# A hybrid backbone step on one core: the first layer's adaLN vectors 2 to 4 on VectorE, the mLSTM gate in another part of Y, another order of the first loads and another last LayerNorm

## The chip, the cores and the metric

The kernel runs on one core of a Trainium2 chip. The core has TensorE (PE; its weight loads are listed apart as PEld), VectorE (DVE), ScalarE (ACT), GpSimd (POOL) and SyncE (SP); each runs its own list of instructions in order and waits on semaphores where data come from another engine or from a transfer. In this kernel SP issues nearly all DMAs, in one order. The metric is the device time of one execution in microseconds.

## The reference, cut to what matters

Two layers (D = 1024) on 640 tokens: 128 prompt tokens and 512 sample tokens, in five tiles of 128 (tile 0 is the prompt). Everything is float32. Shortened from the reference, for one layer:

```
s1, b1, g1, s2, b2, g2 = adaLN(silu(cond))      # 6 vectors of 1024, for 2 conditions
                                                # (prompt, samples): cond @ ada_w + ada_b
h  = x * (1 + scale1) + shift1
aq, ak, av, bq, bk, bv, cq, ck, cv, co, cg = split(h @ w_in)
A  = diff_attention(aq, ak, av)                 # 4 heads, two maps; cached keys and values
B  = neighbourhood / dense attention(bq, bk, bv)  # 4 heads; cached keys and values
C  = head_rms(mLSTM(cq, ck, cv, cg)) * sigmoid(co)  # both directions, 4 heads
x  = layer_norm(ALPHA * x + gate1 * ([A B C] @ w_out))
h  = x * (1 + scale2) + shift2
x  = layer_norm(ALPHA * x + gate2 * (relu(h @ w1)**2 @ w2))
```

The six adaLN vectors of a layer are numbered 0 to 5 here. Vectors 0 and 1 are needed before the first projection of the layer, 2 (the gate of the attention residual) before its out projection, 3 and 4 before the MLP, 5 at the end of the MLP.

## The kernel before, in words

**Products.** A float32 product is made of three matmuls on a high and a low part of each operand (`mul3`, lines 98, 99, 100). Weights come from HBM as chunks of 1 MB into one of two buffers `raw`; ScalarE copies the high part of a quarter (L172) and VectorE subtracts it to get the low part (L117), into one of two or three `wt` slots. The cached keys of group A go the same way (`cak` by DMA, `AK` by L1066 and L117).

**Order.** `layer` writes a plan: a list of `Unit`s, each with a function that emits instructions, a cost in TensorE cycles, and the weight chunks it needs. `weave` merges lists of units in proportion to their costs; `run` walks through the plan and puts chunk loads and splits between the units, in the order in which the plan needs the chunks (`try_dma`, L210). A list scheduler of the language then sets the final order of each engine from the program and its own estimates. So moving one unit moves neighbours on all engines.

**Stages of a layer.** adaLN, the projection of group C, then `c_attn` (mLSTM) woven with `b_proj` (projection of group B), then `a_proj` (projection of group A) woven with `b_attn`, then group A's attention, the out projection, LayerNorm, the MLP in eight chunks of 512 hidden columns, LayerNorm. `Y` is a tile of 128 x 5 x 1024 that is used by all of them in turn: in `c_proj` the mLSTM gate sigmoid(co) is kept in columns 0 to 255 (`sink_o`, `sigm`), `combine` multiplies head outputs `hs` with it into columns 768 to 1023, and `b_attn` loads its own values (from the scratch tensor `s_bv`, L942) and the cached ones (`cbv`, L943) into columns 0 to 511.

**adaLN before.** In layer 0 vectors 0 and 1 are made first of all, by TensorE (`ada_units`: per chunk 16 matmuls of line 380 with `condS` as the moving operand, a copy to `adpart`, 4 picks of line 389, then line 392 on VectorE). Their eight chunks have buffers of their own (`ada`, five of them); `first_units` loads them, the tokens `x`, and the first two `w_in` chunks in four quarters, and multiplies quarter by quarter. Vectors 2 to 4 of layer 0 are twelve more such units, woven into `a_proj` and `b_attn` and the heads behind them. Vector 5 and all of layer 1's are made by VectorE (`ada_dve`, L426: four ops per chunk, each 128 x 1024 by a broadcast row `condB`, summed along the row) between the units of layer 0's MLP.

**The other places.** `rpow` (L127, L128) is a two-step power on GpSimd. `bm` are the six bias tiles of the neighbourhood scores, made on GpSimd (L952) and added on VectorE (L976). `s_aq` is a scratch tensor for the rotated queries of group A (L1090 to L1092 make them, L1116 stores them). In the last layer the final LayerNorm of a token tile is lines 1494 and 1495 (residual), 1366 and 1367 (statistics), `rpow`, 1499 and 1500.

Of the kernel before, what the change touches and what calls it, by code (L numbers as in the profile page):

```python
# [6 lines left out]
F32 = mybir.dt.float32  # L7
F32R = mybir.dt.float32r
AF = mybir.ActivationFunctionType
ALU = mybir.AluOpType  # L10
# [32 lines left out]
PACK = (("abT", (DEPTH, 48)), ("lnT", (DEPTH, 4, KT)), ("ident", (P,)), ("sel2", (2,)),  # L43
        ("cosT", (4, 64)), ("sinT", (4, 64)), ("nmask", (3, 32)), ("gA", (DEPTH,)), ("gC", (DEPTH, 2)))

# [23 lines left out]
class Step:  # L69
# [61 lines left out]
    def w_src(self, k):  # L131
# [4 lines left out]
        if kind == "adt":  # L136
            return d["adaT"][j + (4 if l else -20)]
# [150 lines left out]
    def setup(self):  # L288
# [14 lines left out]
        nc.sync.dma_start(self.condS, d["cond"])  # L303
        pack = self.pack = c.tile([P, d["pack"].shape[1]], F32, name="pack")
# [10 lines left out]
        e = self.adp.tile([P, KT, 32], F32, name="conde", tag="adpart", bufs=2)  # L315
        nc.scalar.activation(e, self.condS, AF.Exp, scale=-1.0)
        nc.vector.tensor_scalar(e, e, 1.0, None, op0=ALU.add)
        nc.vector.reciprocal(e, e)
        nc.vector.tensor_tensor(self.condS, self.condS, e, ALU.mult)


        r, e = (self.adp.tile([P, 2 * D // P], F32, name=n) for n in ("condr", "conre"))
        nc.sync.dma_start(r, d["condr"])
        nc.scalar.activation(e, r, AF.Exp, scale=-1.0)
        nc.vector.tensor_scalar(e, e, 1.0, None, op0=ALU.add)
        nc.vector.reciprocal(e, e)
        nc.vector.tensor_tensor(r, r, e, ALU.mult)
        self.s_cond = tc.dram_tile([2, D], F32, name="s_cond")
        nc.sync.dma_start(self.s_cond.rearrange("j (a b) -> (j a) b", b=2 * D // P), r)

# [20 lines left out]
        self.s_nm = [dt(f"s_nm{l}", [2, H, NTOK]) for l in range(DEPTH)]  # L351

# [17 lines left out]
    def ada_units(self, l, vecs, own=None):  # L370
# [3 lines left out]
        def emit(v, q):  # L374
# [7 lines left out]
            part = self.adp.tile([P, CW], F32, name="adpart", tag="adpart", bufs=2)  # L382
# [20 lines left out]
    def gate_rows(self, l, v):  # L403
# [3 lines left out]
        def rows():  # L407
# [3 lines left out]
            row = self.adp.tile([KT, 2, P], F32, name="grow", tag="adpart", bufs=2)  # L411
# [5 lines left out]
    def ada_dve(self, l, vecs):  # L417
# [3 lines left out]
        def emit(v, q):  # L421
            raw = self.raw[("adt", l, 4 * v + q)].rearrange("p (a b) -> p a b", b=D)
            for b in range(2):
                for j in range(2):
                    x = self.mw.tile([P, D], F32, name="adx", tag="z2", bufs=2)
# [25 lines left out]
    def first_units(self, op, op2, sink_o, sink_q):  # L451
# [5 lines left out]
        def start():  # L457
# [4 lines left out]
            for q in range(4):  # L462
# [7 lines left out]
                if q == 0:  # L470
                    load(self.pack, self.d["pack"])
# [1321 lines left out]
```

## Time and profile before

| | |
|---|---|
| median of three runs | 1839.03 us (1835.86 to 1840.9) |
| the profiled execution | 1840.88 us, its span 1839.0 us, granted clock 0.983 of full speed |
| PE busy | 1743.7 us, 95% of the span |
| DVE busy | 1199.4 us, 65% |
| ACT busy | 709.9 us, 39% |
| POOL busy | 99.4 us, 5% |
| chain that ended last | PE 76%, DVE 13%, DMA 6%, ACT 2%, issue 2% |
| DMA | 240.17 MB, mean 131 GB/s |

The profiled execution took 1.9 us more than its span, and it is the slowest but one of the times shown. An engine's busy time is a sum over stages with different limits. The chain is followed back from the last instruction: at each step to what released it, or to the instruction ahead of it on its engine. Where a stage has PE at its full width in the table of stretches, PE's own list sets that stage; where PE has gaps, the row behind the gap names what it waited for.

### The profile page before, as it was taken

The page shows a single profiled execution, that of the slowest core. Times are in us where ns is not written, and L with a number is a line of the kernel's source. Part 1 is how long each engine was busy: PE and PEld are TensorE (multiplying, and loading weights), DVE is VectorE, ACT ScalarE, POOL GpSimd, SP SyncE. Part 2 cuts the span into 40 slices and gives each one's busy share as a digit, 9 for nine tenths or more (in the row PEclk, how much of TensorE's full clock was granted, in tenths as well). Part 3 has the DMA queues.
Part 4 walks back from the last instruction along what each step waited for, and adds up shares of the span by engine and source line. Part 5 has one row for each costly group of instructions (what it writes and reads, how often), then busy time and mean ns, then how long its engine had stood idle before and what let it go on. Part 6 is the DMA issues. An engine that isn't in the chain of part 4 may idle for free.

```text
span 1839.0 us, 28177 instructions
## 1 busy us (share of the span) xinstructions
PE 1743.7 (95%) x11146; PEld 1582.1 (86%) x11146; DVE 1199.4 (65%) x2270; ACT 709.9 (39%) x1613; POOL 99.4 (5%) x153
## 2 busy tenths in 40 slices
PE   6999899998899999999999999989898999999996
PEld 5999788887899888887989998978788889998895
DVE  3756564788584778778777556769875244444377
ACT  3444234546633222322364423444555332323220
POOL 1103000001000000000010120000010000000001
PEclk9999899999999999999999999989999999999998
DMA  9565545521353534445326655141214122221221
GB/s 357 158 188 164 165 142 173 183 86 58 115 178 120 183 138 153 168 141 196 133 107 198 165 163 148 53 152 52 75 51 171 66 69 92 92 69 69 90 83 58
DMA packets 82389, 240.17 MB, mean 131 GB/s; under 512 B 32001, under 2 KB 43713, under 8 KB 63569
## 3 DMA queue, kind: packets, MB, share of 16 engines
q1 hardware_dynamic: 82256, 238.37, 39.5%
q8 instruction: 87, 1.43, 0.3%
q14 instruction: 46, 0.37, 0.1%
HBM read 211.78 MB, written 26.56 MB: 130 GB/s over the span
## 4 chain that ended last, share of the span: by engine, by line
PE 76%; DVE 13%; DMA 6%; ACT 2%; issue 2%; SPq 1%; POOL 0%; DVEq 0%; ACTq 0%
PE m L98 15%; PE m L100 15%; PE m L99 15%; PE ss L98 6%; PE ss L99 6%; PE ss L100 6%; DVE adx L426 3%; PE m L1204 1%; PE ss L1174 1%; DVE anm L1177 1%; DMA cak<-cak 1%; DVE wt L117 1%; PE m L1014 1%; DMA z<-s_x 1%; DVE Y L1479 1%
## 5 line engine op out<-in xcount | busy, mean ns | idle before, releaser
L98 PE MATMUL m<-wt,Th 128*128 128x256 f32 (+2 forms) x864 | 273.3, 318 | 19.7 <-DVE ry L1091 11.2
L99 PE MATMUL m<-wt,Th 128*128 128x256 f32 (+2 forms) x864 | 268.3, 311 | 1.1 <-DVE wt L117 1.0
L100 PE MATMUL m<-wt,Tl 128*128 128x256 f32 (+2 forms) x864 | 267.1, 312 | 0.2
L117 DVE TENSOR_TENSOR wt<-raw,wt 128x512 fp32r<-128x512 f32 x252 | 167.9, 693 | 74.1 <-ACT wt L172 72.7
L98 PE MATMUL m<-Th,AK 128*128 128x384 f32 (+1 forms) x672 | 208.6, 311 | 5.0 <-DVE Th L112 4.2
L99 PE MATMUL m<-Tl,AK 128*128 128x256 f32 (+1 forms) x672 | 208.1, 311 | 2.2 <-DVE Tl L117 2.2
L172 ACT ACTIVATE wt<-raw 128x512 fp32r<-128x512 f32 x252 | 151.4, 627 | 150.1 <-PE ss L100 87.2
L100 PE MATMUL m<-Th,AK 128*128 128x256 f32 (+1 forms) x672 | 206.6, 311 | 1.8 <-DVE AK L117 1.8
L98 PEld LDWEIGHTS m<-wt,Th 128*128 128x128 f32 x864 | 168.7, 196 | 32.7 <-DVE ry L1091 12.1
L98 PE MATMUL m<-Th,wt 128*128 128x256 f32 (+1 forms) x600 | 186.4, 312 | 3.2 <-DVE rl L1453 3.2
L100 PE MATMUL m<-Th,wt 128*128 128x256 f32 (+1 forms) x600 | 186.5, 311 | 0.0
L99 PE MATMUL m<-Tl,wt 128*128 128x256 f32 (+1 forms) x600 | 186.5, 311 | 0.0
L100 PEld LDWEIGHTS m<-wt,Tl 128*128 128x128 f32 x864 | 168.2, 196 | 9.8 <-issue 1.8
L99 PEld LDWEIGHTS m<-wt,Th 128*128 128x128 f32 x864 | 169.2, 196 | 8.0 <-DVE wt L117 1.5
L426 DVE SCALAR_TENSOR_TENSOR adx<-raw,condB 128x1024 f32<-128x1024 f32 x112 | 131.9, 1218 | 22.0 <-DMA raw<-adaT 22.0
L98 PE MATMUL ss<-wt,hid 128*128 128x512 f32 x356 | 140.9, 396 | 4.9 <-DVE Y L1479 4.9
L100 PE MATMUL ss<-wt,hid 128*128 128x512 f32 x356 | 140.4, 395 | 0.0
L99 PE MATMUL ss<-wt,hid 128*128 128x512 f32 x356 | 140.2, 394 | 0.0
L172 ACT ACTIVATE AK<-raw 128x512 fp32r<-128x512 f32 x140 | 85.2, 628 | 130.7 <-PE ss L100 69.0
L1479 DVE TENSOR_TENSOR Y<-ss,Y 128x1024 f32<-128x1024 f32 x60 | 73.1, 1221 | 94.7 <-PE ss L100 94.7
L1453 DVE SCALAR_TENSOR_TENSOR rl<-m,rl 128x384 f32<-128x384 f32 (+1 forms) x128 | 62.0, 487 | 111.4 <-ACT rl L1452 111.2
L98 PEld LDWEIGHTS m<-Th,AK 128*128 128x128 f32 x672 | 126.2, 188 | 7.8 <-DVE Th L112 5.3
(697 smaller groups left out, 3582.7 us busy)
## 6 DMA issues: line engine op xcount, KB each, us to landing
raw<-w SPq DMA_DIRECT2D x64, 1024.0 KB
raw<-adaT SPq DMA_DIRECT2D x28, 1024.0 KB
raw<-w_in SPq DMA_DIRECT2D x24, 1024.0 KB
raw<-ada SPq DMA_DIRECT2D x12, 1024.0 KB
ada<-ada SPq DMA_DIRECT2D x8, 1024.0 KB
raw<-w_out SPq DMA_DIRECT2D x8, 1024.0 KB
s_x<-Y SPq DMA_DIRECT2D x15, 512.0 KB
hq<-s_cq SPq DMA_DIRECT2D x16, 320.0 KB
```

The source lines that it names most:

```text
L98: mt(out, a[0], b[0], start=first, stop=False)
L99: mt(out, a[0], b[1], start=False, stop=False)
L100: mt(out, a[1], b[0], start=False, stop=last)
L117: self.nc.vector.tensor_tensor(out, x, hi.bitcast(F32), ALU.subtract)
L172: self.nc.scalar.activation(hi, r, AF.Copy)
L426: nc.vector.scalar_tensor_tensor(x, raw[:, b], 1.0, self.condB[:, j], op0=ALU.mult, op1=ALU.mult, accum_out=self.adaF[l][:, v, 2 * q + b, ...
L1014: nc.tensor.matmul(out[64 * i:64 * i + 64], w, rhs, start=b == 0, stop=b == nb - 1)
L1174: nc.tensor.matmul(ps[:, b, :384], qq[i], K[:, j, b * 384:b * 384 + 384], start=i == 0, stop=i == 1)
L1177: nc.vector.tensor_reduce(nm, src, axis=AX.XY, op=ALU.max, negate=True)
L1204: nc.tensor.matmul(hold["o"][:, h * P:h * P + P], aT[:, b * P:b * P + P], V, start=b == 0, stop=b == nk - 1)
L1453: nc.vector.scalar_tensor_tensor(r[:, :n], ps[:, :n], 0.0, r[:, :n], op0=ALU.max, op1=ALU.mult)
L1479: nc.vector.tensor_tensor(y, ps, y, ALU.add)
```

## The change

Six edits.

1. **First loads.** The constants `pack` are split: the adaLN bias and the pick matrix `sel2` (98 columns) are loaded first, the other 806 columns last. The condition comes as 128 x 16 instead of 128 x 256, and `silu` is made on that. In each quarter the second adaLN chunk is loaded right behind the first, ahead of `x` and the `w_in` quarters. The row form of the condition (`condr`, `s_cond`) moves from the start to the end of `first_units`, and its broadcast `condB` is loaded there too, for layer 0's attention, and again in the MLP.
2. **Vectors 2 to 4 of layer 0** are made by VectorE: 48 ops of `ada_dve`, each in a unit of its own, spread over the working units from `c_attn` to the last but twelve of `a_proj` and `b_attn`. The twelve TensorE units are gone.
3. **In the MLP** the same `ada_dve` now returns four units per chunk.
4. **The gate** lies in columns 512 to 767 of `Y`, so that `cbv` and the eight loads of `s_bv` are issued in `b_proj` and no longer at the start of `b_attn`.
5. `bm` has four buffers instead of six.
6. **The last LayerNorm.** In the last layer the residual sum also gives the row sum (`accum_out`), ScalarE squares the centred row and sums it, and VectorE's statistics ops are gone. The last tile's two halves use one pair of PSUM banks (`ss`) instead of two single ones.

```diff
@@ first_units / start
                 if q == 0:
-                    load(self.pack, self.d["pack"])
+                    cond, e = (self.fp.tile([P, KT, 2], F32, name=n) for n in ("cond", "conde"))
+                    load(cond, self.d["cond"])
+                    self.silu(self.condS[:, :, 0:2], cond, e)
+                    load(self.pack[:, :NFIRST], self.d["pack1"])
+                load(own["ada", 0, 4 + q], flat(self.w_src(("ada", 0, 4 + q))))
                 load(x[q], self.d["xT"][:, :, ks])
...
-                load(own["ada", 0, 4 + q], flat(self.w_src(("ada", 0, 4 + q))))
+            load(self.pack[:, NFIRST:], self.d["pack2"])
@@ ada_dve
+        def emit(v, q, b, j):
             raw = self.raw[("adt", l, 4 * v + q)].rearrange("p (a b) -> p a b", b=D)
...
+            x = scratch()
+            nc.vector.scalar_tensor_tensor(x, raw[:, b], 1.0, self.condB[:, j], op0=ALU.mult, op1=ALU.mult,
+                                           accum_out=self.adaF[l][:, v, 2 * q + b, j:j + 1])
@@ c_proj, combine
-            o = Y[:, t, 0:256]
+            o = Y[:, t, 512:768]
...
-            v.tensor_tensor(self.Y[:, :, 768 + c0:832 + c0], hs, self.Y[:, :, c0:c0 + 64], ALU.mult)
+            v.tensor_tensor(self.Y[:, :, 768 + c0:832 + c0], hs, self.Y[:, :, 512 + c0:576 + c0], ALU.mult)
@@ b_proj
+            nc.sync.dma_start(self.Y[:, 4, :512], d["cbv"][l].rearrange("p b c -> p (b c)"))
...
+        def values():
+            src = self.s_bv[l].rearrange("t p c -> (t p) c").rearrange("(b r w) c -> b r w c", b=2, r=4)
+            for c in range(4):
+                w = slice(BLK_START[c], BLK_START[c] + 32)
+                for b in range(2):
+                    nc.sync.dma_start(self.Y[:, c, b * 256:b * 256 + 256], src[b, :, w, :])
@@ b_attn
-            nc.sync.dma_start(Y[:, 4, :512], d["cbv"][l].rearrange("p b c -> p (b c)"))
...
-                b = self.bw.tile([P, 8, 32], F32, name="bm", tag="bm", bufs=6)
+                b = self.bw.tile([P, 8, 32], F32, name="bm", tag="bm", bufs=4)
@@ tail of the last layer
+            v.scalar_tensor_tensor(y, y, 1.0, x, op0=ALU.mult, op1=ALU.add, accum_out=mv[:, 0:1])
+            v.tensor_scalar(mv[:, 0:1], mv[:, 0:1], -1.0 / D, None, op0=ALU.mult)
+            nc.scalar.activation(sq, y, AF.Square, bias=mv[:, 0:1], accum_out=mv[:, 1:2])
+            self.rpow(mv[:, 1:2], mv[:, 1:2], 1.0 / D, 1)
+            v.scalar_tensor_tensor(x, y, mv[:, 0:1], self.rows[:, 0], op0=ALU.add, op1=ALU.mult)
+            v.scalar_tensor_tensor(x, x, mv[:, 1:2], self.rows[:, 1], op0=ALU.mult, op1=ALU.add)
@@ layer
-        ada = self.ada_units(l, (2, 3, 4) if l == 0 else ())
+            todo = self.ada_dve(l, (2, 3, 4), ...)
+            work = [i for i, u in enumerate(X) if u.cost][:-12]
...
+                first = g * len(work) // len(todo)
+                for i, u in enumerate(units):
+                    at[work[min(first + i, len(work) - 1)]] = ... + [u]
```

What it moves, first on SP at the very start of the program, before:

```order
L303 DMA condS<-cond 128x256
L323 DMA condr<-condr 128x16
L469 DMA ada_149<-ada 128x2048
L471 DMA pack<-pack 128x904
L472 DMA x_151<-xT 128x5x256
L473 DMA raw<-w_in 128x512
L475 DMA rawx<-w_gate 128x128
L476 DMA raw<-w_in 128x512
```

and after:

```order
L475 DMA ada_135<-ada 128x2048
L478 DMA cond<-cond 128x16
L480 DMA pack<-pack 128x98
L481 DMA ada_136<-ada 128x2048
L482 DMA x_137<-xT 128x5x256
L483 DMA raw<-w_in 128x512
L485 DMA rawx<-w_gate 128x128
L486 DMA raw<-w_in 128x512
```

The second adaLN chunk, which stood next behind the rows shown of before, is now the fourth load; the tokens and the first weights stand behind it.

On SP where layer 0's `a_proj` begins (`AV`, `cak`: the cached values and keys of group A; `rw`: the position bias of group B), before:

```order
L210 DMA raw<-ada 128x2048
L942 DMA Y<-s_bv_137 128x1x256 x4
L926 DMA rw<-rpbw 128x384 x2
L1053 DMA AV<-cav 128x1024
L1061 DMA cak<-cak 128x512 x2
L942 DMA Y<-s_bv_137 128x1x256 x4
L943 DMA Y<-cbv 128x512
L1116 DMA s_aq_139<-rx 128x256 x2
```

and after:

```order
L937 DMA Y<-s_bv_123 128x1x256 x4
L946 DMA rw<-rpbw 128x384
L629 DMA hq<-s_bq_115 64x1280
L213 DMA raw<-w_in 128x2048
L213 DMA raw<-adaT 128x2048
L946 DMA rw<-rpbw 128x384
L1067 DMA AV<-cav 128x1024
L1075 DMA cak<-cak 128x512 x2
L1130 DMA s_aq_125<-rx 128x256 x2
L1075 DMA cak<-cak 128x512
```

The last four `Y` loads and `cbv` no longer stand between `cak` and `s_aq`; two whole chunks stand ahead of `AV` and `cak`.

On VectorE in layer 0's `c_attn`, behind the mLSTM's decays `dn` (`pt`, `t`, `hs`, `css`: its scores, products, outputs and norms), before:

```order
L801 TENSOR_TENSOR pt<-pt,my 128x128
L844 TENSOR_TENSOR t_1284<-t_1209,dn 128x640
L802 TENSOR_TENSOR pt<-pt,my 128x512
L846 TENSOR_TENSOR hs<-t_1284 128x320
L828 TENSOR_TENSOR t_1419<-m_1504,TK 128x260
L587 SCALAR_TENSOR_TENSOR st<-m_1610,st 128x384
```

and in the same stage after:

```order
L814 TENSOR_TENSOR pt<-pt,my 128x128
L431 SCALAR_TENSOR_TENSOR adx,adaF_82<-raw,condB 128x1024
L804 TENSOR_TENSOR pt<-pt,mz 128x128 x2
L431 SCALAR_TENSOR_TENSOR adx,adaF_82<-raw,condB 128x1024
L599 SCALAR_TENSOR_TENSOR st<-m_1709,st 128x256
L431 SCALAR_TENSOR_TENSOR adx,adaF_82<-raw,condB 128x1024
L840 TENSOR_TENSOR t_1216<-my,TK 128x260
L431 SCALAR_TENSOR_TENSOR adx,adaF_82<-raw,condB 128x1024
```

The four ops of a chunk stand between the ops that feed the mLSTM's next products; 36 of the 48 stand ahead of the first score addition of group B (L976 before), the other 12 behind it.

## Rows read from the trace of the kernel before

**Rows 1.** The page: span, busy time of each engine, and the chain's shares.

```profile
span 1839.0 us, 28177 instructions
PE 1743.7 (95%) x11146; PEld 1582.1 (86%) x11146; DVE 1199.4 (65%) x2270; ACT 709.9 (39%) x1613; POOL 99.4 (5%) x153
PE 76%; DVE 13%; DMA 6%; ACT 2%; issue 2%; SPq 1%; POOL 0%; DVEq 0%; ACTq 0%
```

**Rows 2.** PE's instructions at the start: start, length, count, [idle before, releaser].

```profile
7.12 1.96 PE L380 MATMUL m<-ada,condS 128*32 128x256 f32 x16 [7.12 <-DMA ada<-ada]
...
15.17 1.96 PE L380 MATMUL mw<-ada,condS 128*32 128x256 f32 x16 [4.57 <-DMA ada<-ada]
...
20.48 0.60 PE L98 MATMUL m<-wt,Th 128*128 128x272 f32 x1
```

**Rows 3.** The chain in order of time, start stage: start, length, what.

```profile
5.50 9.63 DMA ada<-ada
...
50.63 1.02 PE mw L380 x16
```

**Rows 4.** Stretches, start stage: length, busy us (count) by engine, granted clock, DMA share, GB/s.

```profile
5.00:40.00 35.00, 25.97 (x181) 19.40 (x181) 12.36 (x32) 10.33 (x21) 3.01 (x4) 0.95 1.03 383
20.00:60.00 40.00, 36.88 (x271) 31.30 (x264) 17.45 (x41) 15.76 (x32) 5.30 (x7) 0.91 0.73 275
```

**Rows 5.** The page's costliest groups: VectorE's adaLN ops in the MLP.

```profile
L426 DVE SCALAR_TENSOR_TENSOR adx<-raw,condB 128x1024 f32<-128x1024 f32 x112 | 131.9, 1218 | 22.0 <-DMA raw<-adaT 22.0
```

**Rows 6.** Stretches of layer 0: c stage (60 to 180), and one of the MLP.

```profile
60.00:180.00 120.00, 120.00 (x906) 116.50 (x905) 81.17 (x182) 55.09 (x144) 22.41 (x28) 1.00 0.62 178
720.00:740.00 20.00, 18.33 (x81) 14.69 (x82) 20.00 (x32) 2.57 (x5) 0.00 (x0) 1.00 0.53 188
```

**Rows 7.** One stretch, line 380's instructions alone: PE busy, PEld busy.

```profile
200.00:345.00 145.00, 15.35 (x192) 6.28 (x192) 0.97 0.56 179
```

**Rows 8.** The same stretch, line 389's alone.

```profile
200.00:345.00 145.00, 6.26 (x48) 6.47 (x48) 0.97 0.56 179
```

**Rows 9.** The chain in order of time, a_proj of layer 0.

```profile
184.41 10.17 DMA cak<-cak
...
195.29 6.91 DMA s_aq<-rx
...
212.59 1.02 PE my L380 x16
```

**Rows 10.** SP's issues there.

```profile
186.38 5.86 SPq L942 DMA_DIRECT2D Y<-s_bv  x4
192.28 2.91 SPq L943 DMA_DIRECT2D Y<-cbv  x1
```

**Rows 11.** PE's instructions there.

```profile
203.03 0.58 PE L98 MATMUL m<-wt,Th 128*128 128x256 f32 x1 [8.01 <-DVE ry L1091]
```

**Rows 12.** The chain in order of time, a_proj of layer 1.

```profile
1092.03 10.88 DMA cak<-cak
...
1103.57 7.23 DMA s_aq<-rx
```

**Rows 13.** Stretches: a_proj of layer 1, and the last PE-bound stretch.

```profile
1090.00:1115.00 25.00, 18.84 (x128) 17.73 (x127) 14.71 (x35) 8.73 (x19) 4.69 (x8) 0.83 0.61 186
1760.00:1804.00 44.00, 44.00 (x250) 39.60 (x249) 29.32 (x40) 13.28 (x26) 0.00 (x0) 1.00 0.21 72
```

**Rows 14.** VectorE's instructions at the end.

```profile
1805.28 1.23 DVE L1495 TENSOR_TENSOR Y<-Y,x 128x1024 f32<-128x1024 f32 x1
1806.54 1.29 DVE L1366 BATCH_NORM_STATS2 st<-Y 128x6 f32<-128x512 f32 x2
...
1831.86 1.28 DVE L1500 SCALAR_TENSOR_TENSOR x<-x,mv,lnrows 128x1024 f32<-128x1024 f32 x1
```

**Rows 15.** GpSimd's instructions at the end.

```profile
1830.05 0.19 POOL L127 TENSOR_SCALAR mv<-mv 128x1 f32<-128x1 f32 x1 [5.17 <-DVE mv L1367]
1831.97 1.23 POOL L127 TENSOR_SCALAR mv<-mv 128x1 f32<-128x1 f32 x1 [1.10 <-DVE mv L1528]
```

More of the change, by code (lines that the diff above doesn't have):

```diff
@@ L302, in setup @@
         self.condS = c.tile([P, KT, 32], F32, name="condS")
-        nc.sync.dma_start(self.condS, d["cond"])
-        pack = self.pack = c.tile([P, d["pack"].shape[1]], F32, name="pack")
+        nc.gpsimd.memset(self.condS, 0.0)
+        pack = self.pack = c.tile([P, sum(math.prod(x) for _, x in PACK)], F32, name="pack")
         at = 0
@@ L351, in setup, with silu, cond_rows, cond_load @@
         self.s_nm = [dt(f"s_nm{l}", [2, H, NTOK]) for l in range(DEPTH)]
+    def silu(self, out, x, e):
+        nc = self.nc
+        nc.scalar.activation(e, x, AF.Exp, scale=-1.0)
+        nc.vector.tensor_scalar(e, e, 1.0, None, op0=ALU.add)
+        nc.vector.reciprocal(e, e)
+        nc.vector.tensor_tensor(out, x, e, ALU.mult)
+    def cond_rows(self):
+        r, e = (self.adp.tile([P, 2 * D // P], F32, name=n) for n in ("condr", "conre"))
+        self.nc.sync.dma_start(r, self.d["condr"])
+        self.silu(r, r, e)
+        self.s_cond = self.tc.dram_tile([2, D], F32, name="s_cond")
+        self.nc.sync.dma_start(self.s_cond.rearrange("j (a b) -> (j a) b", b=2 * D // P), r)
+    def cond_load(self, pool):
+        self.condB = pool.tile([P, 2, D], F32, name="condB")
+        for j in range(2):
+            self.nc.sync.dma_start(self.condB[:, j], self.s_cond[j].partition_broadcast(P))
     def lambdas(self):
@@ L1413, in op @@
             if l == 0:
-                self.condB = self.mw.tile([P, 2, D], F32, name="condB")
-                for j in range(2):
-                    nc.sync.dma_start(self.condB[:, j], self.s_cond[j].partition_broadcast(P))
+                self.cond_load(self.mw)
             self.rows1 = [self.mw.tile([P, D], F32, name=f"rows1{i}") for i in range(2)]
@@ L1560, in layer @@
         P_ += cpr
-        P_ += weave(self.c_attn(l), self.b_proj(l))
+        X = weave(self.c_attn(l), self.b_proj(l))
         ap, ba = self.a_proj(l), self.b_attn(l)
-        P_ += ap[:1] + ba[:2] + ap[1:1 + 5]
+        X += ap[:1] + ba[:2] + ap[1:1 + 5]
         tail = 1 + NT
-        ada = self.ada_units(l, (2, 3, 4) if l == 0 else ())
-        P_ += weave(ap[1 + 5:-tail], ba[2:], ada[:-2])
+        X += weave(ap[1 + 5:-tail], ba[2:])
+        if l == 0:
+            todo = self.ada_dve(l, (2, 3, 4), lambda: self.hp.tile([P, H, PAST], F32, name="adx", tag="ckf", bufs=1).rearrange("p h c -> p (h c)"))
+            work = [i for i, u in enumerate(X) if u.cost][:-12]
+            at = {}
+            for g, units in enumerate(todo):
+                first = g * len(work) // len(todo)
+                for i, u in enumerate(units):
+                    at[work[min(first + i, len(work) - 1)]] = at.get(work[min(first + i, len(work) - 1)], []) + [u]
+            X = [y for i, u in enumerate(X) for y in [u] + at.get(i, [])]
+        P_ += X
         op, cb, oa = self.out_units(l)
```

85 lines of the change are left out of this document (34 added, 51 removed).

## The prediction

> **What bounds the kernel now.** I read the page first. PE is busy for 1743.7 of 1839.0 us and carries 76% of the chain that ended last; VectorE is busy for 1199.4 us and carries 13% of it [rows 1]. So a stage is worth what its PE list gets shorter or what PE's gaps in it get shorter, unless VectorE is full there. The instructions in order of time then show where PE has gaps beside this change: at the start, where it waits for adaLN chunks [rows 2]; where group A's projection begins, in layer 0 [rows 11] and in layer 1 (18.84 busy of 25.00 us [rows 13]); and behind the last MLP product, where VectorE finishes alone [rows 14]. In the mLSTM stage of layer 0 PE has no gap at all: 120.00 of 120 us, with VectorE at 81.17 [rows 6]. The reader should keep those two figures in mind, since most of the new VectorE work is put there.
>
> **The change part by part.** The profiled execution took 1840.88 us, 1.9 more than its span [rows 1] and 1.85 more than the median 1839.03. I work on 1840.9 and take 1.85 off at the end.
>
> *First loads.* Each quarter of the first stage needs two adaLN chunks. The first was there at 7.12, the second only at 15.17 [rows 2]: its transfer was in the queue behind the constants, the tokens and the first weights, and the chain runs through it for 9.63 us [rows 3]. The queue moves 383 GB/s from 5 to 40 us [rows 4], so a chunk of 1.05 MB takes about 2.7 us. With the second chunk behind the first (between them 0.06 MB), it is there at about 7.1 + 2.9 = 10.0 instead of 15.2, and the first product of the projection, at 20.48 before, can start about 5.2 us earlier, once `x` and the first quarter of `w_in` are there as well. Those are now behind 2.1 MB instead of 1.5 MB, so they lose little. The same holds for each later quarter, but not all of it in a sum: the bytes that stand ahead of and with the last adaLN chunk in SP's list (eight chunks, the tokens, the first two weight chunks, constants) are 14.5 MB and were 14.4, at 383 GB/s 38 us plus the first 3, so 41 either way. The last two groups of line 380 ended at 51.65 [rows 3], and there it is PE's own list that sets the time: PE is busy for 36.88 of 40 us from 20 to 60 [rows 4], only 3.1 idle. Starting 5.2 us earlier and with perhaps 1 of the 3.1 gone, I take -6. Bounds: -2 (only the smaller constants help, x and w_in are late in turn) and -11 (5.2 at the front, 3.1 of gaps, and some of the 9% that the clock lacked, 0.91 from 20 to 60).
>
> *Vectors 2 to 4 off TensorE.* Line 380 keeps PE busy for 15.35 us (192 matmuls, 12 chunks x 16 [rows 7]) and line 389 for 6.26 (48 [rows 8]), in stretches where PE has its list full. The chain's row puts 1.02 us on one group of 16 [rows 9], less than 15.35/12 = 1.28, since busy times of pipelined matmuls overlap; by the same ratio the picks are 6.26/12 x 0.8 = 0.42, with their spacing to the neighbours I take 0.52. 12 x (1.02 + 0.52) = 18.5, so -18.5. Bounds: -15 (the picks hidden in gaps) and -21 (all busy time).
>
> *Vectors 2 to 4 onto VectorE.* One op takes 1218 ns in the MLP [rows 5]; the operands have the same form here. 36 of the 48 stand ahead of group B's first score addition, so 36 x 1.218 = 43.9 us go into a stage where VectorE has 120 - 81.2 = 38.8 idle [rows 6]. 81.2 + 43.9 = 125 us of VectorE work in a stage that is now 120 long: VectorE becomes its bound. Without any idle that is +5. VectorE won't be without idle, because its ops are still waiting for ScalarE's copies and for PE's products; I leave it 6 us of the 38.8, so +11. Bounds: 0 (some of the ops slip into the next stage, where VectorE has room) and +44 (each op adds its own length, because the idle falls where the ops don't stand). The nearest row for how VectorE does with such ops is the MLP: from 720 to 740 it is busy for all 20.00 us and PE still for 18.33 [rows 6], so PE loses 8% where VectorE is full, which over 120 us is 10; that is why I stay near the lower end. The other 12 ops fall beside group A's projection and its neighbours, where the groups of lines 380 and 389 also took VectorE's and ScalarE's small ops away: nothing. In the MLP the waits for `adaT` add to 22.0 us over 112 ops [rows 5]; 12 chunks more in layer 0's first half could cost 12/28 of that, 9 us of VectorE waiting, which I count as part of the room up to the upper bound.
>
> A rule speaks against this. One GpSimd op on 128 x 1 took 0.19 us alone and 1.23 while VectorE ran a two-input op [rows 15]. The Trainium skill ("SBUF — State Buffer", section "Who interferes with whom") says that a VectorE instruction with two SBUF inputs contends with a GpSimd instruction that reads SBUF; the trace agrees, 1.23 beside 0.19. Each of the four heads' combines has three GpSimd ops in its chain, so by the rule 12 x 1.04 = 12.5 us more of waits, and by an estimate that puts all of them on the path the sum below would be -15 instead of -27.5. I leave them out of it, since VectorE, not GpSimd, is the full engine there, and keep that inside the range.
>
> *The gate in Y, the value loads.* In layer 0 PE stands idle for 8.01 us before 203.03 [rows 11]. The chain shows why: `cak` was issued at 184.41 and took 10.17, then `s_aq` 6.91 [rows 9]; between the issue of the two SP was held for 5.86 + 2.91 us by the second half of the `Y` loads and `cbv` [rows 10]. Behind the stall come 24 matmuls at half clock, 0.09 us longer each, 2.2 us. All of it is 10.2. The changed order has those loads in `b_proj`, but has put two whole chunks (about 5.5 us of the queue at 383 GB/s) ahead of `AV` and `cak` and another before the last `cak`. So I take -7; bounds 0 (the chunks hold `cak` as long as the loads did) and -10. In layer 1 there is the same picture: `cak` 10.88 and `s_aq` 7.23 on the chain [rows 12], PE idle for 6.2 of 25 us at a clock of 0.83 [rows 13], 6.2 + about 4 for the clock. There no adaLN chunks come in. I take -5, half, for the `cak` transfer itself remains; bounds 0 and -10.
>
> *Four `bm` buffers.* Two bias tiles now wait on GpSimd for group B's first additions, and behind them stands the last mLSTM head's norm. In the plan that head is done by then: 0, bounds 0 and +3 (three GpSimd ops at 1.0 to 1.2).
>
> *The last LayerNorm.* PE's product of a tile pair costs 44 us for 8 tile passes before 1804 [rows 13], some 5.5 each; VectorE needs 1.23 (line 1494) + 1.23 + 1.29 + 0.20 + 1.28 + 1.27 = 6.5 per tile (lines 1495, 1366 and 1500 in [rows 14]; 1494 and 1499 have the same size as 1495 and 1500; 0.20 is the aggregate of 128 x 12). Without the statistics it is 5.0, so VectorE no longer falls behind by 1 us per tile. But ScalarE's square (128 x 1024) and GpSimd's `rpow` come into the tile's chain, and the last tile's first half, which stood ahead of tile 2 on PE, now stands at the end. I take -2; bounds -4 and +2 (that half comes back, 9 matmuls at 0.23).
>
> *The MLPs.* VectorE's order in both is the same as before: 0.
>
> Sum: -6 - 18.5 + 11 - 7 - 5 + 0 - 2 = -27.5. 1840.9 - 27.5 = 1813.4, less 1.85 is about 1812.
>
> **The rivals.**
>
> *B: VectorE takes the ops in its idle time.* Then the term +11 is 0, and PE, full for 120 us before, stays the bound. For it: 38.8 us idle of which 43.9 would need most, and ops that slip 5 us into the next stage. Against it: the MLP row, where a full VectorE does cost PE 8%. 1812 - 11 = 1801; I say 1800.
>
> *C: slower. The ops add one for one.* VectorE runs its list in order. If most of an op's 1.218 us stands ahead of a product's softmax or split that PE waits for, and the idle time stays where it was (waiting for PE's next product), the stage becomes 44 us longer instead of 11. The point from which that decides: when VectorE's idle in the stage stays above 25 of the old 38.8 us, the term is over +30 and the whole no longer faster by more than a few us; with all of it 1812 + 33 = 1845. For it: four ops of a chunk stand within a few instructions (4.9 us), and a scheduler's estimate places them. Against it: PE has other units' work to run meanwhile, the plan mixes two streams there.
>
> *D: the transfers only move.* The stalls in layers 0 and 1 stay (+12), since the chunks stand ahead of `cak`, and VectorE waits for `adaT` at the rate of the MLP (+9 [rows 5]): 1812 + 21 = 1833, with the last tile's half back 1836. For it: SP issues in one order. Against it: the queue moves 178 GB/s in the mLSTM stage [rows 6] and 383 at the start [rows 4], so half of it is free.
>
> **How the numbers follow.** The forecast 0.54, B 0.18, C 0.14, D 0.14. The forecast's own range is 1797 to 1826. A measurement of this kernel tells about 0.3%, 5.5 us, from no change, so faster is below 1833.5: the forecast, B, and a few of D and C, 0.77; within 5.5 us the most of D, 0.09; slower C, 0.14. The range takes in B and D and leaves C's far end out: 1790 to 1838.
>
> **What would show it.** Line 380 has 8 x 16 matmuls, all before 55 us; the first product at about 15; the end of the first stage near 55 instead of 61. From there to group B's first score addition the changed stage takes about 131 us instead of 120, with VectorE at 95% and PE at about 92%; PE at full for 120 would be B, VectorE at 80% in a stage of 160 would be C. The wait before group A's first rotated keys is 1 to 3 us instead of 8, in layer 1 half; if it still reads 8, D. I am wrong if the twelve chunks show waits of VectorE for `adaT` of more than 10 us in that stage.

## The result, and the profile after

The changed kernel takes 1850.64 us (median of four runs, 1847.96 to 1853.03); the kernel before, beside it, 1837.65. The ratio is 1.0068, 95% interval 1.0047 to 1.009: slower by 0.7%, outside the range of the prediction, 1790 to 1838, and on the other side. The profiled execution took 1851.38 us.

The page of the changed kernel: span, busy times, the chain by engine, and the group of the adaLN ops (count | busy, mean ns | idle before, releaser).

```profile
span 1849.5 us, 27779 instructions
PE 1739.9 (94%) x10906; PEld 1583.9 (86%) x10906; DVE 1244.2 (67%) x2353; ACT 712.4 (39%) x1609; POOL 103.6 (6%) x154
PE 70%; DVE 15%; DMA 9%; ACT 4%; issue 2%; SPq 1%; POOL 0%; DVEq 0%; POOLq 0%; ACTq 0%
L431 DVE SCALAR_TENSOR_TENSOR adx<-raw,condB 128x1024 f32<-128x1024 f32 x160 | 191.0, 1222 | 42.3 <-DMA raw<-adaT 41.8
```

PE has 240 matmuls fewer than before and yet only 3.8 us less busy time [rows 1]; its share of the chain fell from 76 to 70%, and DMA's rose from 6 to 9%. The adaLN ops take what the forecast took them to take, 1222 ns [rows 5], but their waits for chunks have gone from 22.0 us over 112 ops to 41.8 over 160.

Where it went is seen by marks. From the end of the first projection (58.8 us, before 60.4) to group B's first score addition (219.2, before 187.0) the stage has grown from 126.6 to 160.4 us, +33.8. From there to the first residual of the out projection, called the second stretch below, the time has shrunk by 11.9, from 148.1 to 136.2 (the residual comes at 355.4, before at 335.1). Layer 1, from the end of its first projection to its first residual, gave back 7.4 us, and the end, from the MLP's last hidden columns on, 3.4. The stretches of the changed kernel: the stage, and both together (length, busy by engine, clock, DMA share, GB/s).

```profile
60.00:219.00 159.00, 141.95 (x955) 135.75 (x953) 120.89 (x252) 54.52 (x143) 24.31 (x26) 0.89 0.67 194
59.00:355.00 296.00, 264.57 (x1929) 249.71 (x1928) 218.06 (x485) 107.55 (x272) 34.05 (x37) 0.91 0.55 164
```

PE, without a gap there before at a clock of 1.00 [rows 6], is idle for 17 of 159 us and has 0.89 of its clock. VectorE is not full: 120.89 of 159, 76%. The forecast named 80% as the sign of its slower rival. How a gap arises is seen in the chain of waits (start, length, what) and in the two engines' instructions behind it.

```profile
172.61 1.22 DVE adx L431 x2
...
173.86 13.55 DMA raw<-adaT
...
187.47 1.11 issue
...
188.67 0.48 DVE pt L813
...
189.19 0.69 PE mx L838 x2
189.88 0.21 PE mz L101
```

```profile
187.44 1.23 DVE L431 SCALAR_TENSOR_TENSOR adx<-raw,condB 128x1024 f32<-128x1024 f32 x1 [7.18 <-DMA raw<-adaT]
...
188.59 0.55 DVE L813 TENSOR_TENSOR pt<-pt,mz 128x384 f32<-128x384 f32 x1
```

```profile
189.19 0.69 PE L838 MATMUL mx<-V,pt 128*128 128x65 f32 x2 [4.51 <-DVE pt L813]
```

The fourth op of a chunk ends at 173.8, only then is the next chunk issued, and its transfer takes 13.55 us. VectorE, out of other work that stands ahead, waits 7.18 us for the first op of that chunk, with the mLSTM's masked scores `pt` behind it, and PE waits 4.51 for `pt`; the matmuls behind the gap are 0.21 us apart, where the same ones stood 0.11 apart at 180: the granted clock from 189.2 to 192.0 is 0.50, the low one of the two levels. VectorE waits six times for a chunk in the stage, 19.5 us together.

The longest gap of PE is another one, at group B's scores:

```profile
225.78 0.77 PE L109 MATMUL mz<-hk,hq 128*128 128x256 f32 x2 [7.55 <-DMA hq<-s_bq]
```

By the chain `hq` is issued only at 214.41: on SP it stands behind the load of `rw` (L946), which is issued when GpSimd has made a bias tile, at 214.0. Run te below, with the same four `bm` buffers but without the VectorE ops, has no such gap.

### The profile page after: what moved, and what is told of

It reads as the page before. It is cut to its first block, busy times and chain, and to the rows that moved or that the text cites. A ratio compares the mean times of both kernels' runs of the same rounds, so it can differ in the third digit from the quotient of the medians.

```text
span 1849.5 us, 27779 instructions
## 1 busy us (share of the span) xinstructions
PE 1739.9 (94%) x10906; PEld 1583.9 (86%) x10906; DVE 1244.2 (67%) x2353; ACT 712.4 (39%) x1609; POOL 103.6 (6%) x154
## 4 chain that ended last, share of the span: by engine, by line
PE 70%; DVE 15%; DMA 9%; ACT 4%; issue 2%; SPq 1%; POOL 0%; DVEq 0%; POOLq 0%; ACTq 0%
PE m L101 13%; PE m L103 13%; PE m L102 13%; PE ss L101 6%; PE ss L102 6%; PE ss L103 6%; DVE adx L431 4%; DMA raw<-adaT 3%; PE ss L1188 2%; DVE wt L120 2%; PE m L1218 2%; DMA s_cq<-st 1%; PE m L1028 1%; DVE Y L1491 1%; ACT pf L1409 1%
## 5 line engine op out<-in xcount | busy, mean ns | idle before, releaser
L431 DVE SCALAR_TENSOR_TENSOR adx<-raw,condB 128x1024 f32<-128x1024 f32 x160 | 191.0, 1222 | 42.3 <-DMA raw<-adaT 41.8
L101 PE MATMUL ss<-wt,hid 128*128 128x512 f32 x360 | 142.4, 396 | 6.0 <-DVE Y L1491 4.5
L103 PE MATMUL ss<-wt,hid 128*128 128x512 f32 x360 | 141.9, 395 | 0.0
L102 PE MATMUL ss<-wt,hid 128*128 128x512 f32 x360 | 141.5, 394 | 0.0
L1491 DVE TENSOR_TENSOR Y<-ss,Y 128x1024 f32<-128x1024 f32 x60 | 73.1, 1222 | 94.9 <-PE ss L103 94.9
```

Source lines behind the costliest of these rows:

```text
L101: mt(out, a[0], b[0], start=first, stop=False)
L102: mt(out, a[0], b[1], start=False, stop=False)
L103: mt(out, a[1], b[0], start=False, stop=last)
L431: nc.vector.scalar_tensor_tensor(x, raw[:, b], 1.0, self.condB[:, j], op0=ALU.mult, op1=ALU.mult, accum_out=self.adaF[l][:, v, 2 * q + b, ...
L1491: nc.vector.tensor_tensor(y, ps, y, ALU.add)
```

## The experiments

All prices are told against run none, the changed kernel without vectors 2 to 4, at 1794.9 us. Vectors 2 to 4 are not the reference's in none, noxfer, shortop, te_nox, nox24k, nox48k, own and own2, each of which leaves out a part of the work. The expectations call two explanations T1 (transfers in front of the ops) and T2 (the length of the ops).

**te: vectors 2 to 4 back on TensorE.**

```diff
-            todo = self.ada_dve(l, (2, 3, 4), ...)     # and the spreading
...
+        ada = self.ada_units(l, (2, 3, 4) if l == 0 else ())
```

> The changed kernel with vectors 2 to 4 of layer 0 made by TensorE again, as before; all its other edits stay. In the changed kernel the stretch from the first projection's end to group B's first score addition took 160.4 us, 126.6 before. If the VectorE ops and their chunks are the cause (theories T1, transfers in front of the ops, and T2, length of the ops), the stretch is back at 125 to 130 us, and with layer 1's shorter wait and the shorter end kept the time is 1822 to 1832. If another edit is the cause (T3: the first loads, the gate's place with its loads, the four bm buffers), the stretch stays over 145 us and the time over 1843.

1827.01 us, ratio 0.9933 (0.9918 to 0.9948). The stage is back at 126.8 us: the VectorE ops and their chunks are the cause of the loss, which is 23.6 us, and the other edits together gain 12.

**noxfer: the ops without the chunks. shortop: the chunks without the ops.**

```diff
-            raw = self.raw[("adt", l, 4 * v + q)]...
+            raw = self.condB if l == 0 and v < 5 else self.raw[...]...      # noxfer
-            ...(x, raw[:, b], 1.0, self.condB[:, j], ...)
+            ...(x[:, :n], raw[:, b, :n], 1.0, self.condB[:, j, :n], ...)    # shortop: n = 2
```

> The changed kernel, but the 48 VectorE ops of layer 0's vectors 2 to 4 read the condition rows in both operands instead of a chunk, and the twelve chunks aren't loaded (these vectors are then not the reference's). The ops keep their 1.22 us. T1 (VectorE stands in front of chunks whose transfer starts only when the chunk before it is used up; 19.5 us of such waits in the trace): the waits are gone, the stretch to group B's first score addition falls from 160 to 130 to 140 us, the time to 1815 to 1828. T2 (the ops' own length, 36 x 1.22 = 44 us, is what lengthens the stretch): it stays above 150 us, the time above 1842.

> The changed kernel, but each of the 48 ops multiplies 2 columns of the chunk instead of 1024 (these vectors are then not the reference's); all twelve chunks are loaded as in the changed kernel and held until the fourth op. T2: 40 of the 44 us of VectorE's work in the stretch go, the stretch is 125 to 130 us, the time 1810 to 1820. T1: VectorE is free earlier and only stands longer in front of each chunk, so the stretch is still 145 us or more and the time above 1835, with more than 19.5 us of waits for the chunks.

noxfer 1840.44 (ratio 1.0024, 0.9999 to 1.005), shortop 1813.92 (0.9863, 0.9848 to 0.9878). Neither theory holds alone: without the twelve chunks the ops still cost 45.5 us, 0.95 us of each 1.22, and with the transfers alone it is 19.0. The two add to 64.5, more than the 55.7 of the changed kernel. In shortop the time has come out as T2 said, but the stage as T1 said: it takes 154.6 us, with 22.1 us of waits for chunks up to 326. One caution on noxfer: since nothing holds the ops there, the scheduler moved them forward, all 48 between 63 and 188 us and ahead of the first score addition (36 in the changed kernel), and the stage takes 170.2 us. So it isn't the same order, and the 45.5 us are no price of the ops at their places.

**dense: the four ops of a chunk behind one unit. late: the ops in the plan's second half.**

```diff
-                    at[work[min(first + i, len(work) - 1)]] = ... + [u]
+                    at[work[first]] = at.get(work[first], []) + [u]                # dense
-            work = [i for i, u in enumerate(X) if u.cost][:-12]
+            work = [i for i, u in enumerate(X) if u.cost and i >= n0][:-4]         # late
```

> The changed kernel with the four ops of a chunk behind one working unit instead of behind four in a row: the chunk's buffer is free three units earlier, and the next chunk has that much more time to arrive before its ops come. T1: the waits for chunks in the stretch fall from 19.5 us to under 12, the time by 5 to 15 us, to 1836 to 1846. T2: 4.9 us of VectorE work in one piece in front of what PE waits for, so the time is the same or up to 10 us longer.

> The changed kernel with the 48 ops spread over the units of group A's projection and group B's attention alone, none in the mLSTM's stage. If an op's price comes from where it stands (in front of the mLSTM's small products, where VectorE feeds TensorE step by step), the first score addition of group B is back near 185 us and the time falls to 1825 to 1838. If the price is that of VectorE's time wherever TensorE's list is full (0.6 to 0.8 us for an op), the loss only moves: 1840 to 1855.

dense 1841.19 (ratio 1.0009, 0.9995 to 1.0023), late 1831.42 (0.9962, 0.9949 to 0.9975). Both are faster than the changed kernel, by 9 and 19 us. In dense the waits for chunks are no shorter (22.7 us up to 345, in the changed kernel 21.3), so its gain isn't the one T1 named, though the time lies in the range given for T1. In late the scheduler still put 20 ops ahead of the first score addition, which came at 203.0, not at 185; place matters, but it was not moved cleanly.

**none: neither ops nor chunks. te_nox: TensorE's units without the chunks.**

```diff
+            if l == 0 and v < 5: ...adaF = abT...; return                          # none
-                 ... self.condS[:, kt, :], raw[:, kt, :], ...
+                 ... self.condS[:, kt, :], raw[:, kt, :] if own else self.pack[:, :CW], ...   # te_nox
```

> The changed kernel without vectors 2 to 4 of layer 0: neither their chunks nor their ops (they are the bias alone, so not the reference's). It gives the price of the work by each engine. With TensorE's units (run te, 1827.0) the difference is the term that the forecast put at 18.5 us, so 1808.5 is expected; if the twelve units stood in gaps of TensorE, 1815 to 1825. Against it stand the short ops with all transfers (1813.9: transfers alone then cost 5 us), and the full ops without transfers (1840.4: ops alone then cost 32 us, 0.66 us of each op's 1.22).

> Run te with TensorE's units of vectors 2 to 4 multiplying a resident table instead of a chunk, and the twelve chunks not loaded (these vectors are then not the reference's). Neither units nor chunks: 1794.9; with both: 1827.0. The matmuls' own time is 21.6 us busy, 18.5 by the chain's rows, so if they cost what they take, 1813 to 1817, and the rest, 10 to 14 us, is the chunks' transfers through the two buffers; if the transfers cost nothing here, 1824 to 1828.

none 1794.93 (ratio 0.9757, 0.9744 to 0.977), te_nox 1825.64 (0.9925, 0.9899 to 0.9951). none lies below both of its forecasts. TensorE's way costs 32.1 us, and its chunks little of that: 30.7 without them. So the twelve units cost more than the 21.6 us that PE is busy with them; in te's trace 26.9 us of it lie in the second stretch, and the rest behind the first residual. The stretch from the first stage to the out projection, in none, in te, and in the changed kernel once more beside noxfer's:

```profile
59.00:305.00 246.00, 242.97 (x1940) 232.60 (x1939) 165.95 (x384) 108.26 (x272) 28.67 (x37) 1.00 0.52 150
```

```profile
57.00:329.00 272.00, 263.50 (x2144) 245.54 (x2143) 169.04 (x398) 112.49 (x289) 29.52 (x37) 0.98 0.59 176
```

```profile
58.00:348.00 290.00, 263.91 (x1933) 249.81 (x1931) 221.66 (x485) 107.93 (x271) 31.34 (x37) 0.91 0.44 127
```

In none PE is busy for 243 of 246 us at a clock of 1.00. The changed kernel runs the same matmuls (1929 recorded, 1940 in none) in 296 us: 28.4 us more of gaps, and 21.6 us more of busy time at a clock of 0.91. So the gaps came with three quarters of their length again in slower matmuls, and noxfer, at 0.91 too, shows the same without the twelve chunks.

**nox24k, nox48k: ops without chunks, held at their places in the plan.**

```diff
+            self.tc.keep_in_program_order(nc.vector.scalar_tensor_tensor(...))
+            if not early or b == 0: ...                                            # nox24k only
```

> As the run without transfers (the VectorE ops read the condition rows, no chunks for vectors 2 to 4), but with every second pair of ops only, 24 instead of 48, and each held at its place in the plan, since the scheduler had moved the ready ops forward. The kernel with neither ops nor chunks takes 1794.9. If VectorE's idle time takes ops up until it is used (the forecast's reasoning: 38.8 us idle in the mLSTM's stage alone, and 24 x 1.22 = 29 us), the time is 1795 to 1803. If an op is paid for almost in full wherever it stands, because TensorE's list waits just behind it, the time is 1816 to 1824 (0.9 to 1.2 us for each).

> The same with all 48 ops, each held at its place in the plan (22 ahead of group B's first score addition instead of 45). Without that hold 48 ops cost 45.5 us over the kernel without ops and chunks. If what counts is how many ops stand in the mLSTM's stage, the wider spread costs 20 to 32 us, 1815 to 1827; if each op has its price anywhere, 38 to 50 us, 1833 to 1845. With 24 ops at 0 to 8 us and 48 at over 30, the idle time absorbs first (convex); with half the price, it is linear.

nox24k 1813.18 (ratio 0.9861, 0.9839 to 0.9882), nox48k 1818.75 (0.9892, 0.9874 to 0.9909). 24 ops cost 18.3 us, 48 cost 23.8, and 48 moved forward cost 45.5: the order alone is worth 21.7 us. By the whole time neither of the two simple rules (free until full, or full price anywhere) holds. nox24k lies between its two forecasts. The stretches by the same marks show where the price arises:

| run | ops ahead of the first score addition | stage, us | matmuls recorded in it | both stretches, us |
|---|---|---|---|---|
| none | 0 of 0 | 127.0 | 966 | 245.4 |
| nox24k | 12 of 24 | 127.0 | 966 | 251.8 |
| nox48k | 24 of 48 | 130.9 | 940 | 263.7 |
| noxfer | 48 of 48 | 170.2 | 939 | 290.3 |
| shortop | 37 of 48, 2 columns each | 154.6 | 1016 | 268.9 |
| kept (below) | 24 of 48, with chunks | 152.6 | 928 | 294.4 |
| changed | 36 of 48, with chunks | 160.4 | 964 | 296.6 |

The stage in none, nox24k, nox48k and kept, and both stretches of nox48k:

```profile
59.00:186.00 127.00, 127.00 (x966) 123.62 (x965) 84.98 (x191) 56.38 (x146) 22.89 (x29) 1.00 0.64 182
59.00:185.00 126.00, 126.00 (x959) 122.69 (x958) 95.97 (x206) 55.37 (x144) 25.41 (x29) 1.00 0.60 174
59.00:189.00 130.00, 125.99 (x933) 121.40 (x932) 107.11 (x227) 55.49 (x145) 25.77 (x26) 0.99 0.58 167
59.00:211.00 152.00, 137.18 (x924) 129.43 (x923) 108.17 (x227) 51.77 (x140) 25.91 (x26) 0.90 0.64 176
59.00:322.00 263.00, 247.65 (x1919) 233.41 (x1918) 218.05 (x483) 106.84 (x270) 35.11 (x37) 0.99 0.47 137
```

In the mLSTM's stage the idle time does take ops that stand at their places and need no chunk: 12 cost nothing there, with PE still at 126 of 126 us, and 24 cost 3.9 us, or about 7 if the 26 matmuls that slipped behind the mark are counted at the stage's 0.13 us each. In the second stretch, where the forecast put 12 ops at nothing, nox24k's 12 cost 6.4 us and nox48k's 24 cost 14.4. Up to the first residual that makes 6.4 and 18.3 us. Behind it, where none of these ops stand, the two traces are 6.3 and 8.5 us longer than none's; executions of one kernel differ by as much (nox24k from 1806.9 to 1817.4), so the stretches are the firmer measure. Nor does every gap lower the clock as much: nox48k has 15.4 us of gaps in 263 at 0.99.

**kept: the changed kernel with that hold. own, own2: chunks in buffers of their own.**

```diff
+            self.tc.keep_in_program_order(nc.vector.scalar_tensor_tensor(...))     # all three
+            self.adr[h] = self.hp.tile([P, D], F32, name="adr", tag="adr", bufs=1)   # own; own2: bufs=2
+            nc.sync.dma_start(self.adr[h], self.w_src(("adt", 0, h // 2))[:, h % 2])
```

> The changed kernel with each of the 48 ops held at its place in the plan by the scheduler's program-order mark; nothing is left out. 24 of them then stand ahead of group B's first score addition instead of 36. If place decides (without chunks the same hold took 45.5 us down to 23.8), and the chunks cost their 19 us (short ops against none: 1813.9 and 1794.9), the time is 1828 to 1840, 10 to 22 us less than the changed kernel. If the waits for the chunks decide, it stays at 1845 to 1852.

> Run kept, but the chunks of vectors 2 to 4 come in halves of 512 KB into one buffer of their own and leave both raw buffers to the weights; the same bytes are loaded, the next half as soon as the second op of the half before is done. To make room the condition's second row isn't loaded and both rows' ops read the first (half of these vectors is then not the reference's). If the two shared buffers are the cause, the splits' waits for w_in fall from 25 us to under 8 and the time to 1818 to 1830. If the queue's time or the order of issue on SP is, it stays at 1838 to 1848.

> Run own with two half buffers, so that the next half is on its way while one is used. To make room the condition's rows aren't loaded at all and each op multiplies the half by itself (vectors 2 to 4 are then not the reference's; the ops keep their 1.22 us and both operands in the same memory). If what costs is that no chunk is in flight while the one before is held, VectorE's waits for halves fall from 41 us to under 10 and the time to 1818 to 1830, that of the ops without chunks (1818.75). If the queue or SP's order is the limit, the waits stay over 25 us and the time over 1838.

kept 1845.42 (ratio 1.0046, 1.0029 to 1.0064), own 1850.51 (1.0059, 1.0039 to 1.0079), own2 1835.22 (0.9994, 0.9978 to 1.0009). Waits of the stretch in kept (who waits for what: us, times, longest), then own's and own2's:

```profile
ACT wt L175 <- DMA raw<-w_in: 25.0, 6, 11.9
DVE adx L431 <- DMA raw<-adaT: 4.1, 1, 4.1
```

```profile
DVE adx L440 <- DMA adr<-adaT: 41.4, 14, 7.4
```

```profile
DVE adx L441 <- DMA adr<-adaT: 13.8, 3, 4.8
```

kept against nox48k is the price of the chunks with the ops held: 26.7 us in the whole time, 30.7 in the two stretches. The wait moves with the buffers. Held to their places the ops hardly wait for chunks, but a chunk then keeps one of the two `raw` buffers, and ScalarE's splits wait 25 us for weights. With one half-size buffer of their own the splits' wait is gone and VectorE waits 41.4; the time lies above both forecasts. With two it waits 13.8 and 15.3 us come back. That is between the two forecasts: with a second buffer in flight about half of the 31.8 us between own and nox48k are gone; what the rest is stays open. own loads one row of the condition, own2 none, and its ops read the half in both operands, so that the two differ by a little more than the buffer.

**pool2: the products on GpSimd, their sums on ScalarE.**

```diff
+                nc.gpsimd.tensor_tensor(x, raw[:, b], self.condB[:, j], ALU.mult)
+                nc.scalar.activation(x, x, AF.Copy, accum_out=...)
```

> The changed kernel with the 48 products on GpSimd (128 x 1024, two inputs) and their row sums on ScalarE, VectorE without them; all chunks loaded, nothing left out. GpSimd's 128 x 256 addition takes 0.65 us alone, so 2.6 to 4 us for one product, 125 to 190 us of an idle engine, ScalarE 48 x 0.9 = 43 us. If only VectorE's list matters: the 1794.9 without ops plus the chunks' 19, 1814 to 1822. By the Trainium skill (SBUF — State Buffer, Who interferes with whom) GpSimd's reads and VectorE's two-input ops shut each other out: then VectorE loses a large part of those 125 to 190 us beside its own two-input work, and GpSimd's small ops of the mLSTM's norms stand behind the products: 1840 to 1880.

1845.46 (ratio 1.0037, 1.002 to 1.0053). GpSimd's group up to 356 us, and one of VectorE's from 60 to 200:

```profile
L432 POOL TENSOR_TENSOR adx<-raw,condB 128x1024 f32<-128x1024 f32 x48 | 117.3, 2444 | 92.7 <-ACT adx L433 72.1 <-DMA raw<-adaT 20.4
```

```profile
L868 DVE TENSOR_TENSOR hs<-hs,css 128x320 f32<-128x320 f32 x3 | 8.0, 2671 | 4.4 <-POOL css L131 4.4
```

The idle engine was little help here, 5 us. A 128 x 320 product of VectorE took 2671 ns on average, and from 60 to 180 of the kernel before:

```profile
L852 DVE TENSOR_TENSOR hs<-hs,css 128x320 f32<-128x320 f32 x3 | 1.7, 559 | 0.9 <-POOL css L128 0.8
```

Each such product of VectorE in layer 0 began within 0.1 us of the start of a GpSimd product and ended 0.35 us after its end. How much of the price this is was not measured apart: the chunks are still loaded, and ScalarE has 48 sums of 1.06 us, for which GpSimd waited 72.1 us.

**gate, start, tail: one edit alone on the kernel before.** The edits are those of the change, nothing else.

> The kernel before with the gate's place in Y and the earlier loads of cbv and s_bv alone. The forecast: 7 us in layer 0 and 5 in layer 1. What run te shows: the wait ahead of group A's first rotated keys in layer 0 is 6.1 us instead of 8.0, since SP stands for 7.3 us in front of the second half of the Y loads, which wait for the s_bv stores, with cak behind them; in layer 1 about 6 us go. So 4 to 9 us less than the kernel before.

> The kernel before with the order and sizes of the first loads alone (the split pack, the small condition, the second chunk of a quarter ahead of the tokens). The forecast was 6 us; in run te the first stage ended 3.6 us earlier, in the changed kernel 1.6. So 2 to 5 us less than the kernel before.

> The kernel before with the new last LayerNorm alone (row sums by the residual addition, ScalarE's square, one bank pair for the last tile). The forecast was 2 us less (bounds 4 less, 2 more); run te ended 3.3 us sooner behind the last MLP product than the kernel before. So 1.5 to 4 us less than before, 1835 to 1837.

gate 1831.7 (ratio 0.9956, 0.9941 to 0.997), start 1839.34 (0.9998, 0.9984 to 1.0012), tail 1836.47 (0.9986, 0.9974 to 0.9998). The first product of start does begin at 15.73 instead of 20.48 [rows 2], and its first projection ends at 57.1 instead of 60.4, but the whole time shows nothing of it. In gate the stall of layer 0 is little shorter (8.01 before [rows 11]):

```profile
203.26 0.58 PE L98 MATMUL m<-wt,Th 128*128 128x256 f32 x1 [6.82 <-DVE ry L1093]
```

and its chain says why: the values are read back from the scratch tensor just stored, and SP stands from 179.8 to 187.3 in front of the second half of these loads, with `cak` behind them.

```profile
178.19 9.08 DMA s_bv<-vb
...
188.53 7.92 DMA Y<-s_bv
...
196.52 5.78 DMA s_aq<-rx
```

**best: te with those loads behind the cached keys.**

```diff
-        return u + [Unit(0, values, soft=True)]
+        self.bvals = Unit(0, lambda: values(1, self.tc.keep_in_program_order), soft=True)
+        return u + [Unit(0, lambda: values(0), soft=True)]          # bvals behind a_proj's first unit; bm has 6 buffers
```

> Run te (the changed kernel with vectors 2 to 4 back on TensorE), with six bm buffers again and the second half of the s_bv loads behind AV and cak on SP in both layers, so that their wait for the s_bv stores no longer holds cak. If that wait sets the stall ahead of group A's first rotated keys (cak issued at 186.4, 4 us behind what released it), the stall of 6.1 us falls to 2 to 4 us and layer 1's by 1 to 4 us: 1819 to 1825 against te's 1827.0. If the release of the memory under AV and cak sets it, the time stays at 1826 to 1828.

1826.06 (ratio 0.9933, 0.992 to 0.9946): no different from te, and like it 0.7% faster than the kernel before and 1.3% faster than the changed one. Both stalls are shorter (4.30 us in layer 0, 6.12 in te; 0.31 in layer 1, 5.35 in te), but the time isn't; why stays open.

```profile
198.25 0.58 PE L101 MATMUL m<-wt,Th 128*128 128x256 f32 x1 [4.30 <-DVE ry L1104]
```

## Why the prediction was wrong, point by point

- **Vectors 2 to 4 onto VectorE, forecast +11, measured +55.7** (1850.6 - 1794.9). This step failed, and beyond its upper bound of 44. The reasoning was that VectorE becomes full, 95% busy in a stage of 131 us, and that all but 6 us of its 38.8 us of idle time take ops. The stage is 160.4 us long with VectorE at 76%. Three parts of the step were wrong. First, it called the waits for the ops' chunks "part of the room up to the upper bound". The transfers cost 19.0 us with ops of 2 columns and 26.7 with the ops held in place, and the waits of VectorE in the stage are 19.5. The sentence that more than 10 us of them would show the prediction wrong was the right one. Second, it counted the ops and not their places. That idle time takes ops was right for 12 held ops without chunks (nothing in the stage) and nearly for 24 (3.9 to 7 us), but the same 48 ops, moved forward by the scheduler, cost 21.7 us more than held. Third, it had no term for the clock: with the gaps it is 0.91 over 296 us, and 21.6 us of the loss is slower matmuls. How the 55.7 us split between chunks and places in the changed kernel's own order stays open, for the parts don't add up.
- **The 12 ops behind the first score addition, forecast 0.** Without chunks, 12 held ops there lengthen the second stretch by 6.4 us (nox24k). In the changed kernel it is 136.2 us, in none 118.4.
- **Vectors off TensorE, forecast -18.5, measured -32.1.** Right in sign, too small and below its bound of -21. The 21.6 us of busy time was in the rows [rows 7, 8]; 5.5 more are gaps (none: 3.0 us idle in 246; te: 8.5 in 272), and some 6 us lie behind the first residual and are not explained. The net of the exchange was forecast at -7.5 and is +23.6: 31 of the 40 us by which the sum missed.
- **First loads, forecast -6, measured 0** (interval -2.9 to +2.2). The second chunk came as early as worked out (the two groups start at 7.07 and 9.02, the first product at 15.62 in the changed kernel), but the first projection ended only 1.6 us earlier there and 3.3 in start. The last adaLN chunk was issued at 37.72, before at 34.48; the prediction's "41 either way" should have bounded the gain. Its 14.4 MB before are, by the sizes in the lists, 13.8.
- **Gate and loads, forecast -12, measured -8** (0.9956). In layer 1 the time from the end of the first projection to the first residual is 3.9 us shorter in gate; in layer 0 the loads read what was just stored, and SP waits 7.5 us for it, nearly as long as the 8.8 that it stood there for the loads. In the changed kernel PE's longest wait for the rotated keys of layer 0 is 0.99 us; that in layer 1 is 3.31, before 3.19.
- **Last LayerNorm, forecast -2, measured -2.6** (0.9986, the interval from 0.9974 to 0.9998). Right: the statistics ops are gone, and GpSimd's first step takes 0.19 us for three of the tiles (0.19 and 1.23 in [rows 15]).

```profile
1822.06 0.19 POOL L130 TENSOR_SCALAR mv<-mv 128x1 f32<-128x1 f32 x1 [422.45 <-ACT sq L1517]
1822.34 0.55 POOL L131 TENSOR_TENSOR mv<-mv,nhalf 128x1 f32<-128x1 f32 x1
```

- **Rivals.** C (each op adds its own length, chance 0.14) came nearest: 1845 was its time, and its test, VectorE's idle time above 25 us, is met with 38 (159 - 120.9). Its mechanism, ops that add their own length, is not what nox48k shows. D's wait for chunks was a second cause, not an alternative. The rule on GpSimd was left out of the sum; in the changed kernel the first `rpow` step took 1.1 us in the first three heads and 0.2 in the last, before 0.6 in the first and 0.2 in the others; with the second step the four heads' grew by 2.7 us in all, of the 12.5 that the rule's estimate gave. The 0.19 us of [rows 15] was not alone either: VectorE ran statistics on a single input beside it, and in the changed kernel a product that reads one operand from PSUM.
- **Four `bm` buffers, forecast 0.** Not tried alone. The gap of 7.55 us at 225.78 stands behind a bias tile, but te has four buffers and no such gap.

## What to carry to other kernels

An engine's idle time in a stage where another engine is full can take new work, but only at the right places: ask for each new op what stands behind it in its engine's list, and who waits for that. Here 48 ops of 1.22 us without chunks cost 18.3 us up to the first residual when each was held at its place, and 44.9 when the scheduler moved them forward, although VectorE had been idle for a third of the stage. When work moves to an engine that needs its own operands, count its transfers and the buffer they sit in as part of the work: here 26.7 us with the ops held. And look at the granted clock behind the gaps in TensorE's list: the changed kernel's 28.4 us of gaps came with 21.6 us of slower matmuls, nox48k, with 12.3 us more of gaps than none, has 4.7 us more of busy time.

## What the runs showed of the hardware that had not been expected

A VectorE op can be held for the length of a GpSimd product. With 48 two-input products of 2.44 us on GpSimd, VectorE's 128 x 320 product went from 559 to 2671 ns, and ended 0.35 us after the GpSimd product each time. The Trainium skill ("SBUF — State Buffer", section "Who interferes with whom") says that a VectorE instruction with two SBUF inputs contends with a GpSimd instruction that reads SBUF; the trace agrees, 2671 ns beside 559.

A whole stretch can lie at a lower mean clock though its longest wait is 7.6 us: 1.00 without the ops, 0.91 with them, with and without the twelve chunks, and 0.99 with the same ops held and no chunks.
